# Hybrid S5 and gated linear attention step on one core: plain Strassen operands through late tiles, and a regrouped third group of sweeps

## The chip, the cores and the metric

The kernel runs on one core of a Trainium2 chip. The metric is the device time of one execution in microseconds (us). TensorE (PE) multiplies, VectorE (DVE), ScalarE (ACT) and GpSimd (POOL) do elementwise work, and SyncE (SP) issues most of the DMAs; each engine works through its own instructions in the order of the program. PEld is the load of a matmul's 128x128 stationary operand, which overlaps the matmul before it.

## The reference

One layer with two token mixers, over 1024 prompt tokens and 64 sample tokens (8 sequences of 8), 1088 in all, D_MODEL = 2048, all in float32:

```python
mod = jax.nn.silu(c) @ w_ada + b_ada
shift, scale, gate = jnp.split(mod, 3, axis=-1)
h = rms_norm(x, norm_gain) * (1 + scale[:, None]) + shift[:, None]
u_a, z_a, q, k, v, z_b, g_lr, m_a, m_b = jnp.split(h @ w_in, SPLIT_POINTS, axis=-1)
a_y, sa_re, sa_im = s5_branch(u_a, ...)      # scan, gelu, times sigmoid(g @ w_glu + b_glu)
a_out = (a_y * jax.nn.silu(z_a)) @ w_a_out
b_y, s_gla = gla_branch(q, k, v, log_a, s0_gla, gla_norm_gain)
b_out = (b_y * jax.nn.silu(z_b)) @ w_b_out
merged = jax.nn.sigmoid(m_a) * a_out + jax.nn.sigmoid(m_b) * b_out
y = x + gate[:, None] * (merged @ w_out)     # then a final rms_norm
```

The branch widths are 1024 each; GLA has 4 heads, each with a state of 128x256 that is carried along the sequence.

## The kernel before

Activations stay in SBUF as features by tokens: `h` is 16 tiles of 128 x 1088, each held as a high and a low part (`hh`, `hl`), and every weight tile is split in the same way (`whi` by ACT, `wlo` by DVE). A product is three matmuls per pair of tiles: high by high, low by high, high by low. Instructions are put on the engines in an order that a scheduler has fixed before the run; buffers come from pools with a fixed number per name, and a pool that is opened in the memory of another has to wait until that other one is free.

The program goes through these stages, with their place in the profiled execution in us from the start of the span:

- 0 to 174: norm, the first two thirds of the conditioning vector `mod` (`ada_chunk`, weight tiles `adaraw` of 512 KB, small matmuls on L203), `modulate`, and the first products of `w_in`.
- 174 to 774: S5, the products for v, q and k. During the k products `blocks` prepares the right-hand operands of a Strassen scheme: sums and differences of quarters of `h` ("t1" to "t4"), made by DVE and ACT in a tile `st` (ring of 3) and written to DRAM by L1076, and the plain quarters "11", "21" and "22", which L1079 and L1080 write to DRAM straight from `hh` and `hl`, one DMA of 272 KB for each part.
- 774 to 1998: `sweeps`. Three groups of eight pairs of output tiles; each group has seven sweeps (a11, a12, s1, s2, s3, a22, s4), each of eight products of 48 matmuls of 128x272 (L1176 to L1178). A sweep loads its operand (`hh`, `hl` from `opscr`) while the sweep before runs. `left` loads the weight tiles `raw`, `wraw` and splits them. Behind this the steps of GLA run (`behind`): four units for the samples and sixteen for the prompt, four heads at each of four stretches of 256 tokens. A unit is the chain L777 (decay), L803 and L833 (scores), L842, L874 (`kT`), L934, L941 and L942 (state and output), L951 (norm), with small operations on DVE and ACT between. `next(self.steps, None)` in the product loop places a step; how often is told by `pace`, one number for each sweep. All stores and the loads of the S5 outputs (`yt`, L993) are issued by POOL, the weight loads by SP.
- 1998 to 2100: `branch_a` (gelu of the S5 outputs, `w_glu`).
- 2100 to 2495: `merge` (`w_a_out`, `w_b_out`, 32 products), with the last third of the conditioning (`ada_gates`, weight tiles `gateraw`, L203) stepped between its products.
- 2495 to the end: `final` (`w_out`, residual, norm).

Of the kernel before, what the change touches and what calls it, by code (L numbers as in the profile page):

```python
# [10 lines left out]
F32 = mybir.dt.float32  # L11
F32R = mybir.dt.float32r
U8 = mybir.dt.uint8
AF = mybir.ActivationFunctionType
# [4 lines left out]
P = 128  # L19
# [5 lines left out]
T = TS + TP  # L25
CH = [(0, 320), (320, 384), (704, 384)]
HT = T // 2
# [3 lines left out]
QK4 = 512  # L31


class Hybrid:
# [946 lines left out]


    def stage(self, name):
        return self.p2.tile([P, T], F32, tag="st", name=name, bufs=6)

    def gelu_y(self, i):
        nc = self.nc
# [77 lines left out]
    def blocks(self, h):  # L1065

        nc = self.nc
        V = nc.vector
        with ExitStack() as ctx:
            pp = self.pool("blocks", ctx=ctx)  # L1070

            def split(name, k, v):
                st = pp.tile([P, T], F32R, tag="st", name="st", bufs=3)
                nc.scalar.activation(st[:, :HT], v, AF.Copy)
                V.tensor_tensor(st[:, HT:], v, st[:, :HT].bitcast(F32), ALU.subtract)
                nc.gpsimd.dma_start(self.opscr[name][k], st.bitcast(F32))  # L1076
            for k in range(8):
                for name, (hi, lo), o in (("11", h[8 + k], 0), ("21", h[k], 0), ("22", h[k], HT)):
                    nc.gpsimd.dma_start(self.opscr[name][k][:, :HT], hi[:, o:o + HT].bitcast(F32))  # L1079
                    nc.gpsimd.dma_start(self.opscr[name][k][:, HT:], lo[:, o:o + HT].bitcast(F32))  # L1080
                x, y = (pp.tile([P, T], F32, tag=n, name=n, bufs=2) for n in "xy")
                yield
                V.tensor_tensor(x, h[8 + k][0].bitcast(F32), h[8 + k][1].bitcast(F32), ALU.add)
                V.tensor_tensor(y, h[k][0].bitcast(F32), h[k][1].bitcast(F32), ALU.add)
                b11, b12, b21, b22 = x[:, :HT], x[:, HT:], y[:, :HT], y[:, HT:]
                V.tensor_tensor(b11, b12, b11, ALU.subtract)
                split("t1", k, b11)
                yield
                V.tensor_tensor(b12, b22, b12, ALU.subtract)
                split("t3", k, b12)  # L1090
                V.tensor_tensor(b11, b22, b11, ALU.subtract)
                split("t2", k, b11)
                yield
                V.tensor_tensor(b21, b11, b21, ALU.subtract)
                split("t4", k, b21)
# [37 lines left out]
    def sweeps(self, w, groups, h):  # L1133

        nc = self.nc
# [12 lines left out]
        count = [0, 0]  # L1148

        def raws():  # L1150
            i = count[0] % 10
            count[0] += 1
            if i > 7:
                return self.wp.tile([P, QK4], F32, tag="wraw", name="wraw", bufs=2)
            return rawv[i]

        def fin():
            count[1] += 1
            return finv[count[1] % 8]
        n = 0  # L1160
        for g, group in enumerate(groups):
            for r, (an, bn) in enumerate(self.SWEEPS):
                B, N = sets[n % 2], sets[(n + 1) % 2]
                n += 1
                nxt = self.SWEEPS[r + 1][1] if r < 6 else "11" if g + 1 < len(groups) else None
                for i, (pair, dst, silu) in enumerate(group):
                    ps = self.pmm.tile([P, 2, 512], F32, tag="mm2", name="mm", bufs=2)
                    for q in range(2):
                        hi, lo = self.left(w, an, pair, q, self.wscr[i], raws)
                        for k in range(4):  # L1170
                            c = slice(k * P, (k + 1) * P)
                            bhi, blo = B[4 * q + k]
                            for m in range(2):
                                o = ps[:, m, :NC]
                                bh, bl = bhi[:, m * NC:(m + 1) * NC], blo[:, m * NC:(m + 1) * NC]
                                nc.tensor.matmul(o, hi[:, c], bh, start=q + k == 0, stop=False)  # L1176
                                nc.tensor.matmul(o, hi[:, c], bl, start=False, stop=False)  # L1177
                                nc.tensor.matmul(o, lo[:, c], bh, start=False, stop=q == 1 and k == 3)  # L1178
                            if 4 * q + k in ((), (4,), (2, 6), (1, 4, 6))[self.pace[r]]:
                                next(self.steps, None)  # L1180
                    if nxt:
                        right(nxt, i, N[i])
# [115 lines left out]
    def run(self):  # L1298
        nc, a = self.nc, self.a
# [22 lines left out]
        h = []  # L1322
# [34 lines left out]
        self.pmmctx.close()  # L1357
        self.pmm = self.pool("pmm2", space=PSUM, ctx=self.pmmctx)
        self.steps = self.behind()
        self.pace = (3, 2, 2, 2, 1, 3, 2)  # L1360
        pairs = lambda j0, d, silu=False: [((j0 + i, j0 + i + 1), (d[i], d[i + 1]), silu) for i in range(0, len(d), 2)]
        self.sweeps(w, [pairs(40, self.mas), pairs(56, self.mbs), pairs(8, self.zas, True) + pairs(32, self.zbs, True)], h)
        for _ in self.steps:
# [3 lines left out]
        self.p2ctx = ExitStack()  # L1367
        self.p2 = self.pool("p2", ctx=self.p2ctx)
        aa = self.branch_a()
        self.steps = self.ada_gates()  # L1370
        self.ticks = ()
        self.merge(aa)
        for _ in self.steps:
            pass
        self.final()


# [74 lines left out]
```

## Time and profile before

| | |
|---|---|
| time, median of 3 runs | 2922.17 us (2920.47 to 2926.75) |
| profiled execution | 2938.97 us, span 2937.2 us, mean granted clock 0.982 |
| PE busy | 2813.0 us, 96% of the span |
| PEld busy | 2669.6 us, 91% |
| DVE, ACT, POOL busy | 58%, 35%, 14% |
| DMA | 610.52 MB moved, mean 208 GB/s |

The clock is the rate that the throttle granted to TensorE as a share of full speed: 1.00 is 2.4 GHz, and 1.2 GHz is the other level. A busy share is the mean of the stages, which have different limits. In the windows of the rows below each line gives a stretch, its length, then busy time and count of PE, PEld, DVE, ACT and POOL, then the granted clock, the share of the 16 DMA engines and GB/s. All times of the trace are those of the one profiled execution.

### The profile page before, as it was taken

How to read it: one execution, taken by the hardware profiler on the slowest of the kernel's cores; microseconds unless marked ns; L12 is line 12 of the kernel's file. 1: busy time of each engine (PE TensorE's matmuls, PEld its weight loads, DVE VectorE, ACT ScalarE, POOL GpSimd, SP SyncE). 2: the span in 40 equal slices, each digit the busy share in tenths (PEclk: the TensorE clock that was granted, in tenths of full speed). 3: DMA queues.
4: the chain of work that ended last, by engine and by line, in shares of the span. 5: the costliest groups of instructions: out<-in, count | busy, mean ns of one | idle time of the engine just before them, and what ended most of it. 6: DMA issues, size and time to landing. Idle time of an engine off the chain costs nothing.

```text
span 2937.2 us, 54282 instructions
## 1 busy us (share of the span) xinstructions
PE 2813.0 (96%) x20736; PEld 2669.6 (91%) x20736; DVE 1715.7 (58%) x4016; ACT 1018.9 (35%) x1823; POOL 411.5 (14%) x702
## 2 busy tenths in 40 slices
PE   7999999999899999999999989999999999899987
PEld 4689899999888999998999989999988999899987
DVE  3486777678245786667777535656532322456465
ACT  4222222223233344444344442333221211344434
POOL 1101222121001100011000032011110000203021
PEclk9999999999899999999999999999999999999999
DMA  9944444447668887668867599953575433555455
GB/s 377 386 132 133 117 127 122 114 122 258 235 206 288 295 298 255 187 217 302 292 219 246 194 276 296 319 181 123 173 257 176 136 120 118 184 161 181 145 181 164
DMA packets 321748, 610.52 MB, mean 208 GB/s; under 512 B 47952, under 2 KB 106096, under 8 KB 321360
## 3 DMA queue, kind: packets, MB, share of 16 engines
q1 hardware_dynamic: 256624, 433.51, 46.4%
q0 software_dynamic: 48528, 158.70, 15.6%
q10 hardware_dynamic: 16336, 14.84, 1.5%
q8 instruction: 163, 2.67, 0.4%
q14 instruction: 97, 0.79, 0.1%
HBM read 465.65 MB, written 132.87 MB: 204 GB/s over the span
## 4 chain that ended last, share of the span: by engine, by line
PE 63%; DMA 18%; DVE 8%; issue 7%; ACT 3%; POOL 1%; SPq 1%; DVEq 0%; POOLq 0%; ACTq 0%
PE mm L71 12%; PE mm L72 12%; PE mm L73 12%; PE mm L1178 6%; PE mm L1177 6%; PE mm L1176 6%; DMA raw<-in_w_in_dram 5%; DMA wraw<-in_w_in_dram 2%; DMA hh<-opt 1%; DMA bz<-zbs 1%; DMA raw<-ws 1%; DMA wraw<-in_w_out_dram 1%; PE bg L203 1%; DVE wlo L58 1%; DVE wlo L1130 1%
## 5 line engine op out<-in xcount | busy, mean ns | idle before, releaser
L1176 PE MATMUL mm<-hh,whi 128*128 128x272 f32 x2688 | 788.9, 293 | 25.4 <-ACT whi L1128 13.1
L1178 PE MATMUL mm<-hh,wlo 128*128 128x272 f32 x2688 | 790.2, 294 | 1.6 <-DVE wlo L1130 1.6
L1177 PE MATMUL mm<-hl,whi 128*128 128x272 f32 x2688 | 785.6, 292 | 0.0
L71 PE MATMUL mm<-ahi,whi 128*128 128x384 f32 (+3 forms) x1656 | 547.6, 331 | 17.9 <-DVE y L1248 9.0
L73 PE MATMUL mm<-ahi,wlo 128*128 128x384 f32 (+3 forms) x1656 | 544.2, 329 | 0.6 <-DVE wlo L58 0.4
L72 PE MATMUL mm<-alo,whi 128*128 128x384 f32 (+3 forms) x1656 | 543.5, 328 | 0.0
L1176 PEld LDWEIGHTS mm<-hh,whi 128*128 128x128 f32 x2688 | 514.3, 191 | 31.3 <-ACT whi L1128 14.7
L1178 PEld LDWEIGHTS mm<-hh,wlo 128*128 128x128 f32 x2688 | 513.8, 191 | 5.2 <-DVE wlo L1130 2.4
L1177 PEld LDWEIGHTS mm<-hl,whi 128*128 128x128 f32 x2688 | 514.3, 191 | 3.1 <-issue 1.0
L58 DVE TENSOR_TENSOR wlo<-wraw,whi 128x512 fp32r<-128x512 f32 x368 | 269.5, 740 | 269.8 <-ACT whi L56 268.4
L56 ACT ACTIVATE whi<-wraw 128x512 fp32r<-128x512 f32 x368 | 230.3, 630 | 490.5 <-PE mm L72 278.4
L71 PE MATMUL mm<-hh,whi 128*128 128x384 f32 (+3 forms) x1056 | 344.2, 329 | 9.0 <-ACT hh L266 9.0
L72 PE MATMUL mm<-hl,whi 128*128 128x384 f32 (+3 forms) x1056 | 346.8, 329 | 2.8 <-DVE hl L268 2.8
L73 PE MATMUL mm<-hh,wlo 128*128 128x384 f32 (+2 forms) x1056 | 346.6, 330 | 0.0
L71 PEld LDWEIGHTS mm<-ahi,whi 128*128 128x128 f32 x1656 | 314.6, 190 | 35.2 <-issue 22.8
L73 PEld LDWEIGHTS mm<-ahi,wlo 128*128 128x128 f32 x1656 | 314.5, 190 | 3.9 <-DVE wlo L58 2.5
L72 PEld LDWEIGHTS mm<-alo,whi 128*128 128x128 f32 x1656 | 315.0, 190 | 1.3 <-issue 0.4
L1128 ACT ACTIVATE whi<-raw 128x512 fp32r<-128x512 f32 x270 | 168.6, 628 | 323.3 <-PE mm L1177 191.6
L1130 DVE TENSOR_TENSOR wlo<-raw,whi 128x512 fp32r<-128x512 f32 x270 | 183.9, 684 | 51.4 <-ACT whi L1128 48.6
L71 PEld LDWEIGHTS mm<-hh,whi 128*128 128x128 f32 x1056 | 198.4, 189 | 14.2 <-ACT hh L266 11.5
L72 PEld LDWEIGHTS mm<-hl,whi 128*128 128x128 f32 x1056 | 198.9, 189 | 9.9 <-DVE hl L268 4.7
L73 PEld LDWEIGHTS mm<-hh,wlo 128*128 128x128 f32 x1056 | 198.8, 189 | 3.4 <-issue 2.6
(373 smaller groups left out, 3446.1 us busy)
## 6 DMA issues: line engine op xcount, KB each, us to landing
raw<-in_w_in_dram SPq DMA_DIRECT2D x346, 256.0 KB
wraw<-in_w_out_dram SPq DMA_DIRECT2D x192, 256.0 KB
wraw<-in_w_in_dram SPq DMA_DIRECT2D x182, 256.0 KB
adaraw<-in_w_ada_dram SPq DMA_DIRECT2D x64, 512.0 KB
hl<-opt SPq DMA_DIRECT2D x96, 272.0 KB
hh<-opt SPq DMA_DIRECT2D x96, 272.0 KB
raw<-ws SPq DMA_DIRECT2D x78, 256.0 KB
ws<-raw POOLq DMA_DIRECT2D x77, 256.0 KB, 5.5
```

Source lines behind the costliest of these rows:

```text
L56: nc.scalar.activation(hi, raw, AF.Copy)
L58: nc.vector.tensor_tensor(lo, raw, hi.bitcast(F32), ALU.subtract)
L71: nc.tensor.matmul(ps, hi[:, c], ah[:, sl], start=start, stop=False)
L72: nc.tensor.matmul(ps, hi[:, c], al[:, sl], start=False, stop=False)
L73: nc.tensor.matmul(ps, lo[:, c], ah[:, sl], start=False, stop=stop)
L203: self.nc.tensor.matmul(ps[i:i + 32, :256], self.c32[:, k, :], raw[:, (k - k0) * 256:(k - k0 + 1) * 256], start=k < 4, stop=k >= KT - 4, t ...
L1128: nc.scalar.activation(hi, x, AF.Copy)
L1130: nc.vector.tensor_tensor(lo, x, hi.bitcast(F32), ALU.subtract)
L1176: nc.tensor.matmul(o, hi[:, c], bh, start=q + k == 0, stop=False)
L1177: nc.tensor.matmul(o, hi[:, c], bl, start=False, stop=False)
L1178: nc.tensor.matmul(o, lo[:, c], bh, start=False, stop=q == 1 and k == 3)
```

## The change

Three things change. In `blocks` the plain quarters are copied by ACT into a tile of the ring `st` (two copies each) and written by one DMA of 544 KB, where two DMAs read the activations before. In `sweeps` the pace becomes one list per group; ahead of the third group all GLA steps that are left are drained, and a pool "more" is opened with 12 more weight tiles (`raw2`) and two `gateraw` tiles; in the third group the steps are those of `ada_gates`, in the sweeps a11, a12 and a22; ahead of its last sweep the pool is closed, and the pool of `stage` tiles, in which the S5 outputs are loaded, comes after it. The merge no longer steps anything. The ring of `stage` tiles grows from 6 to 7.

```diff
     def stage(self, name):
-        return self.p2.tile([P, T], F32, tag="st", name=name, bufs=6)
+        return self.p2.tile([P, T], F32, tag="st", name=name, bufs=7)
...
             for k in range(8):
-                for name, (hi, lo), o in (("11", h[8 + k], 0), ("21", h[k], 0), ("22", h[k], HT)):
-                    nc.gpsimd.dma_start(self.opscr[name][k][:, :HT], hi[:, o:o + HT].bitcast(F32))
-                    nc.gpsimd.dma_start(self.opscr[name][k][:, HT:], lo[:, o:o + HT].bitcast(F32))
+                for name, hl, o in (("11", h[8 + k], 0), ("21", h[k], 0), ("22", h[k], HT)):
+                    st = pp.tile([P, T], F32R, tag="st", name="st", bufs=3)
+                    for p in range(2):
+                        nc.scalar.activation(st[:, p * HT:(p + 1) * HT], hl[p][:, o:o + HT].bitcast(F32), AF.Copy)
+                    nc.gpsimd.dma_start(self.opscr[name][k], st.bitcast(F32))
...
         def raws():
-            i = count[0] % 10
             count[0] += 1
+            if sp and count[0] % 2:
+                return sp.tile([P, QK4], F32, tag="raw2", name="raw2", bufs=12)
+            i = (count[0] // 2 if sp else count[0]) % 10
...
+            last = g + 1 == len(groups)
+            if last:
+                for _ in self.steps:
+                    pass
+                sctx = ExitStack()
+                sp = self.pool("more", ctx=sctx)
+                self.p2 = sp
+                self.steps = self.ada_gates()
+            pace = ((1, 2, 2, 2, 2, 3, 2), (3, 3, 2, 2, 2, 3, 2), (2, 2, 0, 0, 0, 1, 0))[g]
...
+                if last and r == 6:
+                    for _ in self.steps:
+                        pass
+                    sp = None
+                    sctx.close()
...
-                            if 4 * q + k in ((), (4,), (2, 6), (1, 4, 6))[self.pace[r]]:
+                            if 4 * q + k in ((), (4,), (2, 6), (1, 4, 6))[pace[r]]:
                                 next(self.steps, None)
...
-        self.pace = (3, 2, 2, 2, 1, 3, 2)
...
         aa = self.branch_a()
-        self.steps = self.ada_gates()
-        self.ticks = ()
         self.merge(aa)
-        for _ in self.steps:
-            pass
```

Three places of the instruction order show what moves. The first is TensorE before the change, at the border between the second group's last sweep (s4, tile `mm_19823`) and the third group's first (a11, tile `mm_19918`); the names `hh`, `hl`, `whi` and `wlo` are sweep operands, `on`, `gr` and `q` belong to GLA:

```order
L1178 MATMUL mm_19823<-hh_1532,wlo_19865 128x272
L1176 MATMUL mm_19918<-hh_1126,whi_19920 128x272
...
L1178 MATMUL mm_19918<-hh_1284,wlo_19922 128x272
L1176 MATMUL mm_19918<-hh_1284,whi_19920 128x272
L1177 MATMUL mm_19918<-hl_1285,whi_19920 128x272
L951 MATMUL bg_19347<-on_19308,ones_h_8747 128x256
L777 MATMUL bg_19360<-gr_19361,wgu_8755 128x256
L803 MATMUL bg_19405<-q_19180,k_19181 32x32 x8
L1178 MATMUL mm_19918<-hh_1284,wlo_19922 128x272
```

The first sweep of the third group follows at once, and the last units of GLA stand among its matmuls. The second is the same border on TensorE after the change (s4 ends with `mm_19836`, a11 begins with `mm_19907`):

```order
L1197 MATMUL mm_19836<-hh_1532,wlo_19874 128x272
L934 MATMUL bg_18152<-v_17473,kT_18111 128x256 x2
...
L951 MATMUL bg_18238<-on_18198,ones_h_8818 128x256
L777 MATMUL bg_18251<-gr_18252,wgu_8826 128x256
...
L951 MATMUL bg_18701<-on_18675,ones_h_8818 128x256
L777 MATMUL bg_18714<-gr_18715,wgu_8826 128x256
...
L951 MATMUL bg_19144<-on_19118,ones_h_8818 128x256
L777 MATMUL bg_19157<-gr_19158,wgu_8826 128x256
...
L951 MATMUL bg_19712<-on_19673,ones_h_8818 128x256
L1195 MATMUL mm_19907<-hh_1126,whi_19910 128x272
```

Seventy rows, all of GLA, now stand between the two sweeps: the end of one unit (from L934) and three whole ones (L777 to L951), with no matmul of a sweep between them. The third place is the queue of SP after the change, at the same border (`o2_204`, `o3_205` are GLA's outputs in DRAM, `on` the tile that is stored, `raw2` the new weight tiles; the brackets name the semaphores that a row waits for):

```order
L956 DMA o2_204<-on_19154 256x1x256 [waits DMAHW3_49,DVE_49]
L945 DMA out_2_dram<-St3_11393 128x256 [waits DMAHW4_49,DVE_49]
L956 DMA o3_205<-on_19722 256x1x256 [waits DMAHW5_49,DVE_49]
L1106 DMA raw2_19908<-in_w_in_dram 128x512 [waits DMAHW4_49,DMAHW3_49,DMAHW5_49,DMAHW2_49,DMAHW6_49,DMAHW1_49,DMAHW7_49,DMAHW0_49,Activation_49]
...
L1106 DMA raw2_19980<-in_w_in_dram 128x512
...
L965 DMA gateraw_20008<-in_w_ada_dram 128x1024 [waits DMAHW2_49,PE_49]
L965 DMA gateraw_20044<-in_w_ada_dram 128x1024 [waits DMAHW3_49,PE_49]
...
L1106 DMA raw2_21058<-in_w_in_dram 128x512 [waits DMAHW6_49,DVE_49]
```

The third group's first weight load stands behind the store of GLA's last output and waits for all eight DMA semaphores; the later `gateraw` loads wait for PE with weight loads behind them.

## Rows read from the trace of the kernel before

**Rows 1.** The page's part 4: the chain that ended last, by engine.
```profile
PE 63%; DMA 18%; DVE 8%; issue 7%; ACT 3%; POOL 1%; SPq 1%; DVEq 0%; POOLq 0%; ACTq 0%
```

**Rows 2.** Windows, 20 to 160 us: busy us, clock, DMA share, GB/s.
```profile
60.00:80.00 20.00, 18.29 (x132) 12.94 (x132) 6.96 (x18) 3.95 (x5) 4.27 (x8) 1.00 1.02 405
...
sum 140.00, PE 122.91 PEld 79.72 DVE 62.28 ACT 41.98 POOL 23.72; mean PE 17.56 PEld 11.39 DVE 8.90 ACT 6.00 POOL 3.39
```

**Rows 3.** Line L1080, the second of the two copy DMAs of `blocks`.
```profile
L1080 POOL DMA_DIRECT2D op<-hl x24: 540/540/542, 51.1 to 172.8; - x24
```

**Rows 4.** Windows of 20 us around the start of the sweeps.
```profile
780.00:800.00 20.00, 14.57 (x89) 11.35 (x88) 7.48 (x30) 7.82 (x19) 1.63 (x3) 0.74 0.52 162
800.00:820.00 20.00, 13.53 (x71) 11.56 (x72) 7.32 (x22) 7.68 (x16) 0.32 (x1) 0.70 0.48 147
```

**Rows 5.** Line L1076, the other DMAs of `blocks`.
```profile
L1076 POOL DMA_DIRECT2D opt<-st x32: 531/531/561, 673.4 to 747.8; - x32
```

**Rows 6.** Line L1074, the copy on ScalarE ahead of each of them.
```profile
L1074 ACT ACTIVATE st<-x x24: 643/659/662, 670.9 to 742.6; 128x544 fp32r<-128x544 f32 x24
```

**Rows 7.** Windows: the first sweep, the second group, the third group.
```profile
774.00:855.80 81.80, 69.90 (x474) 62.52 (x473) 29.82 (x91) 31.11 (x67) 1.95 (x4) 0.83 0.54 168
...
1205.60:1623.30 417.70, 402.59 (x3981) 388.43 (x3980) 294.45 (x724) 189.83 (x386) 41.32 (x73) 0.99 0.75 248
1623.30:1998.20 374.90, 353.90 (x2845) 350.04 (x2844) 205.98 (x339) 142.39 (x201) 70.79 (x130) 0.98 0.78 250
```

**Rows 8.** Timeline of the last GLA unit: start, duration, engine, line, operation, idle before.
```profile
1634.10 0.59 PE L951 MATMUL bg<-on,ones_h 128*128 128x256 f32 x2
...
1658.90 0.38 ACT L876 ACTIVATE kT<-bg 128x256 f32<-128x256 f32 x1 [2.39 <-PE bg L874]
...
1661.69 1.02 PE L934 MATMUL bg<-v,kT 128*128 128x256 f32 x4
...
1663.65 0.48 DVE L943 SCALAR_TENSOR_TENSOR St<-St,eb,bg 128x256 f32<-128x256 f32 x1 [2.64 <-PE bg L942]
...
1666.54 0.38 PE L942 MATMUL bg<-q,St 128*128 128x128 f32 x2
...
1668.14 0.74 POOL L948 TENSOR_TENSOR on<-on 128x256 f32<-128x256 f32 x1 [36.37 <-ACT on L947]
...
1671.21 0.59 PE L951 MATMUL bg<-on,ones_h 128*128 128x256 f32 x2
...
1677.70 0.69 DVE L955 TENSOR_TENSOR on<-bg,rsn 128x512 f32<-128x512 f32 x1
...
1678.42 0.52 SPq L956 DMA_DIRECT2D o<-on  x1
```

**Rows 9.** Page, parts 5, 6: a weight split; a DMA, us to landing.
```profile
L1128 ACT ACTIVATE whi<-raw 128x512 fp32r<-128x512 f32 x270 | 168.6, 628 | 323.3 <-PE mm L1177 191.6
...
ws<-raw POOLq DMA_DIRECT2D x77, 256.0 KB, 5.5
```

**Rows 10.** Windows: sweeps a11, s1, a22 and s4 of the third group.
```profile
1623.30:1680.60 57.30, 57.30 (x541) 55.93 (x540) 30.63 (x74) 27.31 (x52) 2.01 (x3) 1.00 0.51 170
...
1737.30:1793.60 56.30, 50.51 (x384) 50.12 (x385) 24.82 (x38) 21.24 (x24) 20.54 (x39) 0.94 0.97 289
...
1898.50:1946.80 48.30, 48.30 (x387) 48.30 (x386) 24.90 (x38) 15.38 (x24) 3.78 (x7) 1.00 0.73 244
1946.80:1998.20 51.40, 48.43 (x386) 47.86 (x385) 38.74 (x54) 27.53 (x31) 13.97 (x25) 1.00 0.51 157
```

**Rows 11.** Windows: 14 products of the merge with gates, 14 without.
```profile
2099.50:2303.00 203.50, 197.70 (x1282) 174.81 (x1282) 72.86 (x113) 45.36 (x59) 19.51 (x37) 0.98 0.65 219
2303.00:2469.00 166.00, 166.00 (x1009) 166.00 (x1008) 49.83 (x77) 32.48 (x42) 11.08 (x21) 1.00 0.36 116
```

**Rows 12.** Groups by line, 2099.5 to 2303 us: the gates' matmuls.
```profile
L203 PE MATMUL bg<-gateraw,c 128*32 128x256 f32 x256 | 22.1, 397 | 2.9 <-DMA gateraw<-in_w_ada_dram 2.9
```

**Rows 13.** Line L993, the loads of the S5 outputs.
```profile
L993 POOL DMA_DIRECT2D yt<-y x64: 528/531/896, 1683.3 to 1987.6; - x64
```

More of the change, by code (lines that the diff above doesn't have):

```diff
@@ L1164, in sweeps @@
                 n += 1
+                if last and r == 6:
+                    for _ in self.steps:
+                        pass
+                    sp = None
+                    sctx.close()
                 nxt = self.SWEEPS[r + 1][1] if r < 6 else "11" if g + 1 < len(groups) else None
```

## The prediction

> **What bounds the kernel now.** I read the chain that ended last first, then windows of stages, then the rows around the places that change. The chain is TensorE for 63% and DMA for 18% of the span [rows 1]; an edit pays only where TensorE waits or runs work of low value, and costs only where it makes TensorE wait. Four such places are touched. In the first stage the 16 DMA engines are full (share 1.02, 405 GB/s from 60 to 80 us), yet PE is busy 122.9 of the 140 us from 20 to 160 [rows 2]. At the start of the sweeps PE is busy 14.6 and 13.5 of 20 us, at a clock of 0.74 and 0.70 [rows 4]; this first sweep takes 81.8 us [rows 7]. A sweep without disturbance takes 48.3 us, as a22 of the third group shows, while s1 takes 56.3 at a DMA share of 0.97 and a11 57.3 with GLA in it [rows 10]. In the merge 14 products with gates between them take 203.5 us, 14 without take 166.0 [rows 11].
>
> **The change, part by part.** The sum is made against the profiled 2938.97 us, which is 16.8 us above the median of the runs; I carry the difference over to the median unchanged.
>
> *Early copies gone.* L1080 issues 24 DMAs from 51.1 to 172.8 us [rows 3], L1079 as many in the same way. Each moves 0.279 MB; spread evenly, some 27 of the 48 lie before 120 us, 7.5 MB, or 19 us of the DMA engines at 405 GB/s. But PE stands idle only 140 − 122.9 = 17.1 us there [rows 2], and part of that is the chain of modulation, which no DMA shortens. Gain between 0 and 17; I take 12.
>
> *Late copies.* 48 copies of 0.66 us [rows 6] go to ACT, 31.6 us, beside a PE that works through the k products; ACT has room. The ring is what paces them: 32 uses took 673.4 to 747.8 us, 2.40 us each [rows 5]. At that pace 56 uses end at about 673 + 55 × 2.4 = 805 instead of 748. Behind it on ACT stand the weight splits of the first sweep's second product, and the pool that GLA needs opens later. So PE stalls some 17 us between 780 and 805; but it already loses 5.4 + 6.5 us there, and part of its clock, to the first GLA units, which now start later [rows 4]. One stall takes the place of the other: 0, between −10 and +15. GLA loses about 40 us of cover, though.
>
> *GLA out of the third group.* The second group takes 417.7 us [rows 7], 79.6 over seven sweeps of 48.3; it holds most of the units. The new paces place about as many steps in the two groups together as before (248 against 240), and since they start later, nearly as many units get done: −3, between −8 and +2.
>
> *The drain.* This is the decisive part. The order of TensorE after the change has the end of one unit and three whole ones between the second and the third group, without a sweep matmul among them; before, they lay among the products of a11. So the third group can't start until GLA has run through by itself, at the speed of its own chain over DVE, ACT and PE. The nearest rows are those of the last unit before: from one L951 at 1634.1 to the next at 1671.2, 37.1 us [rows 8]. In that time its small matmuls stood in PE's queue behind sweep matmuls: `kT` was ready at 1659.28 and L934 began at 1661.69 (2.4 us); the state at 1664.13, L942 at 1666.54 (2.4); POOL's result at 1668.88, L951 at 1671.21 (2.3). Without these 7.1 us it takes 30.0. Four weight splits of 0.63 us on ACT [rows 9] lie in its way too, which leaves 27.5; more waits of the first kind lie earlier in the unit, while a slower clock (below) would lengthen its matmuls. I take 25, between 22 and 30. The end of the first unit, L934 to L951, was 9.5 us, less two waits of 4.7: 5. Behind the last L951 comes the norm until the output is ready, 1671.21 to 1678.39, 7.2 us [rows 8]; then its store, then the first `raw2` load, which waits for that store, then a split of 0.63. A DMA of this size takes 5.5 us to land among others [rows 9]; for the pair I take 7.5, between 4 and 11. So the drain costs 5 + 3 × 25 + 7.2 + 7.5 + 0.6 = 95 us, between 5 + 66 + 12 = 83 and 5 + 90 + 19 = 114. Nothing covers it: PE, with 96% busy elsewhere, has only these matmuls.
>
> A rule of the Trainium skill bears on the pair of transfers: "DMA: Bandwidth & Descriptors", section "Anatomy of one DMA — SWDGE (gpsimd) path", gives about 2.0 us plus the bytes over 436 GB/s, an estimate of 2.6 us for 256 KB and 5.2 for the pair. The row's 5.5 us for one is twice that, in traffic; by the page the sum would be 2.3 us smaller.
>
> *Third group.* Before: 374.9 us [rows 7]. After, seven sweeps at 48.3 are 338; the gates' matmuls, 22.1 us [rows 12] and an estimated 3 for their transposes, move in: 363. Of the 8 us that s1 lost at a DMA share of 0.97 [rows 10], and the sweeps before and after it likewise, I keep half, 12 or 13: the S5 loads leave, the gates' 16.8 MB come. That is 376, +1 to +2, taken as +2, between −10 and +25.
>
> *S5 outputs late.* The 64 loads, 0.53 us of POOL each [rows 13], were spread from 1683 on. Now all 34 us of them stand in or behind a last sweep of 51.4 us [rows 10], the last ones behind the sweep's stores, and the gelu and splits behind them; `branch_a` runs k-outer, and needs the last tiles late. +3, between 0 and +15.
>
> *Merge.* 203.5 − 166.0 = 37.5 us [rows 11], of which 22.1 are the gates' matmuls [rows 12] and 5.8 PE's idle time; the rest is what lies around small matmuls. The branch's loads may still stall. −34, between −24 and −37.5.
>
> Sum: −12 + 0 − 3 + 95 + 2 + 3 − 34 = +51. On the median: 2922 + 51 = **2973**.
>
> **The rivals.** *The drain is short.* The three units belong to three heads and share no data, so their work on DVE and ACT could overlap. Against it: in the order each L777 stands behind the L951 of the unit before, and the chain starts at L777. The other parts give −44 together, so the kernel is faster by more than 0.2% (5.8 us, about what a measurement here tells from no change) once the drain costs under 38; with units of 5 us it is 5 + 15 + 15 = 35, and the time 2913; with none left it is 2878.
>
> *The third group becomes bound by DMA.* It moved 250 GB/s for 374.9 us [rows 7], 94 MB; without the S5 loads (4.5 MB) and with the gates it is 106 MB. At s1's 289 GB/s for 0.97 [rows 10], 298 at full share, this takes 356 us, just below the 376 allowed; on SP, a `gateraw` load that waits for PE holds the weight loads behind it, with only 12 more tiles as cover. If it decides, +25 instead of +2: 2996.
>
> *The drain at the lower clock.* With PE busy some 14 of 20 us the granted clock was 0.70 to 0.74 [rows 4], a mix of 2.4 and 1.2 GHz. The drain leaves PE far less busy, so its matmuls could all run at 1.2 GHz: units of 30 us, a drain of 110, time 2988. The Trainium skill warns of this in "TensorE: Matmul & The Clock Gate", section "HAM oscillation — how this bites in real kernels": waits between bursts of matmuls cost the clock at the start of each burst. By that page this rival is the likelier course within my range of units; the trace shows the lower clock at such a place, but no drain.
>
> *The early copies weren't in the way.* If stage one is held by PE and modulation alone, the first term is 0: 2985.
>
> **How the numbers follow.** The forecast with its own range, 2950 to 2995, has 0.58; it holds the last two rivals. The third group bound by DMA, or several costs at their upper ends, 2995 to 3025, has 0.17. A drain somewhat shorter, or gains at their bounds, 2928 to 2950, has 0.08. Within 0.2%: 0.05. Faster: 0.12. Slower is 0.83. The bounds, added in squares (drain 17, copies early 9 and late 13, third group 18, the rest 14), give some 32 us to each side; with the rival of DMA above and part of the short drain below, 2918 to 3012 holds 8 in 10.
>
> **What would show it.** Between the second and the third group a stretch of some 95 us in which PE holds only GLA's lines, at a low clock. Units of about 25 us from L951 to L951. The first `raw2` load some 8 us ahead of the first a11 matmul, and behind the last GLA store. The merge at about 11.9 us a product from the start. Stage one at about 162 instead of 174 us. L1076 ending past 800, the first sweep about as long as before. The prediction is wrong if the drain is under 50 us, if DMA is at full share throughout the third group, or if stage one or the first sweep moves by more than 20.

## The result and the profile after

The changed kernel takes 2962.39 us (2961.43 to 2966.74, 4 runs) against 2922.76 of the kernel before: a ratio of 1.0137, 95% interval 1.0119 to 1.0155. It is slower by some 40 us, where 51 were forecast.

The windows of the stages after the change (columns as in the rows ahead of the prediction): the first sweep; the rest of the first two groups; the gap; the third group; `branch_a`; the merge.

```profile
761.10:829.60 68.50, 55.86 (x410) 54.51 (x409) 24.46 (x61) 29.05 (x58) 6.42 (x12) 0.88 0.77 263
829.60:1594.90 765.30, 743.37 (x6890) 710.83 (x6890) 514.19 (x1240) 315.86 (x631) 79.22 (x143) 0.99 0.79 263
1594.90:1691.40 96.50, 33.90 (x424) 26.19 (x422) 51.10 (x157) 40.22 (x85) 3.42 (x5) 0.60 0.20 71
1691.40:2065.40 374.00, 368.61 (x2959) 349.38 (x2960) 188.41 (x298) 119.64 (x176) 55.09 (x102) 0.99 0.81 275
2065.40:2162.70 97.30, 96.33 (x580) 95.25 (x579) 61.58 (x64) 37.49 (x51) 20.58 (x38) 1.00 0.47 140
2162.70:2543.10 380.40, 380.08 (x2306) 379.47 (x2305) 145.53 (x198) 87.61 (x110) 42.54 (x73) 1.00 0.45 145
```

The first profile of the kernel before lay 16 us above its usual runs, so I had it profiled again (below); that second profile, with a span of 2924.6 us, is the one to compare with. Its windows, in the same order, without a gap:

```profile
778.10:856.80 78.70, 69.45 (x474) 62.07 (x473) 29.87 (x91) 30.96 (x67) 1.95 (x4) 0.85 0.56 172
856.80:1616.60 759.80, 743.39 (x7091) 712.98 (x7091) 534.02 (x1295) 332.96 (x667) 80.42 (x144) 1.00 0.80 264
1616.60:1989.90 373.30, 353.21 (x2845) 349.62 (x2844) 206.58 (x339) 142.61 (x201) 70.72 (x130) 0.99 0.78 251
1989.90:2085.80 95.90, 95.44 (x579) 95.15 (x578) 55.76 (x59) 26.13 (x46) 6.44 (x12) 1.00 0.35 114
2085.80:2499.50 413.70, 409.33 (x2578) 386.63 (x2577) 144.44 (x215) 91.33 (x118) 42.20 (x72) 1.00 0.52 171
```

(In the first profile of the kernel before the merge ran from 2094 to 2511 us, not from 2100 to 2495 as the list of stages ahead of the prediction has it.)

So the 40 us are a sum of large terms: the sweeps start at 761.1 instead of 778.1 (−17.0), the first sweep −10.2, the rest of the first two groups +5.5, the gap +96.5, the third group +0.7, `branch_a` +1.4, the merge −33.3; `final` is shorter by 3. The gap is a stretch that was not there before: TensorE is busy 33.9 of 96.5 us, at a mean granted clock of 0.60.

One unit of GLA in the gap, on TensorE (start, duration, engine, line, operation, idle before and what ended it):

```profile
1599.86 1.22 PE L951 MATMUL bg<-on,ones_h 128*128 128x256 f32 x2 [1.55 <-POOL on L948]
1600.52 0.77 PE L777 MATMUL bg<-gr,wgu 96*128 96x256 f32 x1
...
1612.29 0.73 PE L833 MATMUL bg<-g 128*32 128x16 f32 x32 [10.63 <-DVE g L820]
...
1619.79 2.07 PE L934 MATMUL bg<-v,kT 128*128 128x256 f32 x4 [0.47 <-ACT kT L876]
...
1626.62 0.83 PE L951 MATMUL bg<-on,ones_h 128*128 128x256 f32 x2 [1.55 <-POOL on L948]
1626.97 0.69 PE L777 MATMUL bg<-gr,wgu 96*128 96x256 f32 x1
```

From one L777 to the next are 26.5 us. Two fifths of it are one wait: from L803 to L833 TensorE stands for 10.6 us until DVE and ACT have made the decays. L934, 1.02 us in [rows 8], takes 2.07 here, at the lower clock. Over a whole unit, from one L951 to the next, TensorE's GLA matmuls took 6.23 us before, at a granted clock of 1.00:

```profile
1634.10:1671.20 37.10, 6.23 (x133) 5.07 (x134) 4.38 (x14) 1.92 (x4) 1.00 0.33 97
```

In the gap they take 10.45, at 0.55 (both windows count the instructions on GLA's tile `bg` alone, and have no column for POOL):

```profile
1626.62:1653.18 26.56, 10.45 (x134) 8.06 (x134) 4.39 (x14) 1.93 (x4) 0.55 0.09 29
```

TensorE's waits over the whole gap (us, times, longest):

```profile
PE bg L833 <- DVE g L820: 36.5, 9, 10.7
PE mm L1195 <- ACT whi L1130: 12.0, 1, 12.0
```

The second line is the way out. It is seen in the chain that ended last (start, duration, what): norm of the last output, its store, then the load, then the first split and the first matmul.

```profile
1678.66 0.71 PE bg L951 x2
...
1683.40 0.70 DVE on L955
1684.12 2.41 DMA o<-on
1687.13 3.56 DMA gateraw<-in_w_ada_dram
1690.69 0.63 ACT whi L1130
```

The last L951 ends the GLA work at 1678.66; the output is ready at 1684.1, the first new weight tile is issued when its store has landed, at 1686.7, and TensorE goes on at 1691.4: 12.7 us. (The chain names a `gateraw` load, issued right behind the first weight tile; the split reads the weight tile, so I take the wait to be for that.) The list of stages has all stores issued by POOL; these stores of GLA's outputs are issued by SP, so the last of them and the first weight load stand in one queue.

In the first stage the DMA engines are no longer full from 60 us on:

```profile
60.00:80.00 20.00, 18.67 (x131) 12.38 (x125) 6.57 (x16) 3.22 (x5) 0.00 (x0) 1.00 0.89 352
...
sum 140.00, PE 125.09 PEld 84.91 DVE 67.96 ACT 44.45 POOL 0.00; mean PE 17.87 PEld 12.13 DVE 9.71 ACT 6.35 POOL 0.00
```

They stood at a share of 1.02 before [rows 2]. The copies that took the place of the early DMAs, and the end of `blocks`:

```profile
L1081 ACT ACTIVATE st<-hh x24: 639/658/662, 651.9 to 774.0; 128x544 fp32r<-128x544 f32 x24
```

```profile
L1076 POOL DMA_DIRECT2D opt<-st x32: 531/531/542, 660.3 to 788.3; - x32
```

The last one starts at 788 us, where it was 748 [rows 5]. In the first sweep TensorE waits twice for weight splits, 5.5 and 7.2 us:

```profile
PE mm L1195 <- ACT whi L1130: 12.6, 2, 7.2
```

The first of these splits, at 775.07, stood behind the copies on ACT. For the second ACT itself was idle, until a weight tile had landed, from loads that SP issued from 776.4 us on, behind a wait of 6.5 us for the splits before:

```profile
790.70 1.17 ACT L1130 ACTIVATE whi<-raw 128x512 fp32r<-128x512 f32 x2 [3.42 <-DMA raw<-in_w_in_dram]
```

At that time the DMA engines were full, and TensorE had nothing to do:

```profile
784.00:791.00 7.00, 0.21 (x2) 0.00 (x0) 0.72 (x1) 0.96 (x2) 0.53 (x1) 0.74 1.03 417
```

So one wait is ACT's order, the other the load on the DMA engines; whose transfers filled them was not taken apart, but with the early copies both waits go (below).

The third group loads more than before, and TensorE hardly waits; its sweep s1:

```profile
1812.20:1861.60 49.40, 49.40 (x394) 48.84 (x393) 26.47 (x41) 10.77 (x17) 9.18 (x17) 1.00 0.99 366
```

The S5 outputs are loaded from 2010 us on, and were from 1683 [rows 13]:

```profile
L993 POOL DMA_DIRECT2D yt<-y x64: 528/531/793, 2009.8 to 2083.1; - x64
```

The merge runs its 32 products at the pace of those without gates in [rows 11], 11.9 us each.

### The profile page after: what moved, and what is told of

It is laid out like the page before. It is cut to its first block, busy times and chain, and to the rows that moved or that the text cites. A ratio compares the mean times of both kernels' runs of the same rounds, so it can differ in the third digit from the quotient of the medians.

```text
span 2964.8 us, 54310 instructions
## 1 busy us (share of the span) xinstructions
PE 2805.0 (95%) x20736; PEld 2672.4 (90%) x20736; DVE 1728.4 (58%) x4016; ACT 1043.8 (35%) x1867; POOL 398.3 (13%) x678
## 4 chain that ended last, share of the span: by engine, by line
PE 62%; DMA 12%; issue 8%; DVE 7%; ACT 3%; POOL 2%; SPq 0%; DVEq 0%; POOLq 0%; ACTq 0%
PE mm L71 11%; PE mm L73 11%; PE mm L72 11%; PE mm L1195 8%; PE mm L1197 8%; PE mm L1196 8%; DMA raw<-in_w_in_dram 4%; DMA wraw<-in_w_in_dram 2%; DMA wraw<-in_w_out_dram 1%; DMA bz<-zbs 1%; DVE wlo L1132 1%; DVE wlo L58 1%; POOL yt L993 1%; DMA hh<-opt 1%; DVE s L295 1%
## 5 line engine op out<-in xcount | busy, mean ns | idle before, releaser
L71 PE MATMUL mm<-hh,whi 128*128 128x384 f32 (+2 forms) x1056 | 344.1, 329 | 4.0 <-ACT hh L266 4.0
L1130 ACT ACTIVATE whi<-raw 128x512 fp32r<-128x512 f32 x283 | 177.1, 629 | 427.8 <-PE mm L1196 349.4
L1132 DVE TENSOR_TENSOR wlo<-raw,whi 128x512 fp32r<-128x512 f32 x283 | 193.0, 686 | 133.3 <-ACT whi L1130 91.6
```

Source lines behind the costliest of these rows:

```text
L71: nc.tensor.matmul(ps, hi[:, c], ah[:, sl], start=start, stop=False)
L1130: nc.scalar.activation(hi, x, AF.Copy)
L1132: nc.vector.tensor_tensor(lo, x, hi.bitcast(F32), ALU.subtract)
```

## The experiments

Ratios are to the kernel before, run on the same chip as the experiment in question; its medians there were 2926.6 to 2927.9 us.

**The kernel before, once more** (no edit).

> The kernel before, unchanged, profiled a second time. The two profiles differ by 27.6 us of span while the medians of the runs differ by 39.6, so some 12 us of the first profile of before are not in its usual runs. Theory 1: they lie in its first sweep, which took 81.8 us there; a second profile shows that sweep at about 68 to 70 us, as after the change, and a span of some 2922. Theory 2: they are spread over the whole program (clock); then the first sweep takes 81 to 82 us again and every stage is a little shorter.

Time 2926.43, span 2924.6; the first sweep took 78.7 us, as the second group of windows above shows. Theory 1 falls: the first profile was 4 us faster ahead of the sweeps, 12 slower in them and 3 in the merge, so its excess has no one place, as theory 2 has it in part. The comparison of stages above is with this profile.

**Only the plain operands** (in the kernel before, the edit to `blocks` alone, as in the diff of the change).

> The kernel before with the change to the plain operands alone. Theory 1 (the early copies held the first stage, the late ones are hidden): the start of the sweeps moves from 774 to 761 us, the first sweep stays at what it is in the second profile of before, and the time is 2923 - 13 = 2910. Theory 2 (the late copies give it back in the first sweep, whose weight splits stand behind them on ScalarE, and in GLA, which starts some 30 us later): 2923 to 2930.

Ratio 0.9997 (0.9983 to 1.0012): no change, though the sweeps start at 760.6. The windows are the first sweep, the rest of two groups, the third group:

```profile
760.60:844.90 84.30, 63.94 (x442) 58.46 (x443) 31.47 (x87) 36.74 (x70) 6.48 (x13) 0.86 0.71 231
844.90:1607.40 762.50, 742.88 (x6989) 712.68 (x6988) 526.47 (x1268) 322.16 (x652) 80.40 (x143) 0.99 0.79 264
1607.40:1988.10 380.70, 360.50 (x2977) 355.64 (x2977) 220.33 (x388) 152.76 (x228) 71.75 (x131) 0.98 0.78 249
```

Of the 17.5 us won ahead of the sweeps, 5.6 go in the first sweep, 2.7 in the rest of two groups and 7.4 in the third, where GLA, which began later, ends later: its last L951 stands at 1695 us instead of 1665, and the S5 loads, which wait for its memory, begin at 1712 instead of 1676. Theory 2.

**The change with early copies.**

```diff
-                for name, hl, o in (("11", h[8 + k], 0), ("21", h[k], 0), ("22", h[k], HT)):
-                    st = pp.tile([P, T], F32R, tag="st", name="st", bufs=3)
-                    for p in range(2):
-                        nc.scalar.activation(st[:, p * HT:(p + 1) * HT], hl[p][:, o:o + HT].bitcast(F32), AF.Copy)
-                    nc.gpsimd.dma_start(self.opscr[name][k], st.bitcast(F32))
+                for name, (hi, lo), o in (("11", h[8 + k], 0), ("21", h[k], 0), ("22", h[k], HT)):
+                    nc.gpsimd.dma_start(self.opscr[name][k][:, :HT], hi[:, o:o + HT].bitcast(F32))
+                    nc.gpsimd.dma_start(self.opscr[name][k][:, HT:], lo[:, o:o + HT].bitcast(F32))
```

> The changed kernel with the plain operands written early, straight from the activations, as before the change. Theory 1 (the late copies save 13 to 18 us before the sweeps; they gave it back in the other experiment only because GLA, which starts later, held memory longer; here GLA runs out in the gap either way): 2962 + 15 = 2977. Theory 2 (GLA's earlier start shortens the gap): 2962 or less.

Ratio 1.0116 (1.0091 to 1.0142), not to be told from the change's 1.0137. Both theories fail, the second by its mechanism, though its time is met: the gap is as long as before (1595.5 to 1691.9), and the 14 us that the early copies cost ahead of the sweeps come back at once in the first sweep:

```profile
775.50:830.60 55.10, 52.99 (x417) 51.28 (x418) 17.23 (x44) 21.15 (x44) 1.63 (x3) 0.97 0.59 186
```

55.1 us instead of 68.5: this is the 12.6 us wait for the splits, gone (1.4 us are left). The late copies move a cost, they don't remove it.

**The paces alone** (the kernel before with the change's numbers for the first two groups).

```diff
         for g, group in enumerate(groups):
+            pace = ((1, 2, 2, 2, 2, 3, 2), (3, 3, 2, 2, 2, 3, 2), (3, 3, 3, 2, 1, 3, 2))[g]
...
-                            if 4 * q + k in ((), (4,), (2, 6), (1, 4, 6))[self.pace[r]]:
+                            if 4 * q + k in ((), (4,), (2, 6), (1, 4, 6))[pace[r]]:
```

> The kernel before with the paces of the change in the first two groups (GLA goes on at three steps a product in the third). Theory 1 (it is the lighter pace of the first sweep, one step a product instead of three, that made this sweep 13 to 24 us shorter): the first sweep falls from 79 to about 55 us, the third group grows by one more unit, some 9 us, and by later S5 loads, and the time falls by about 10, to 2915. Theory 2 (the first GLA units cost the same wherever they stand): no change.

Ratio 1.0075 (1.0058 to 1.0093), slower, which neither theory allowed. The profiled run lies 7 us under the median. First sweep, rest of two groups, third group:

```profile
777.50:850.10 72.60, 63.89 (x444) 58.37 (x443) 25.77 (x76) 30.54 (x65) 1.95 (x4) 0.86 0.57 178
850.10:1620.10 770.00, 748.50 (x6894) 716.90 (x6893) 514.41 (x1222) 314.86 (x623) 80.26 (x143) 0.98 0.78 260
1620.10:2002.20 382.10, 364.22 (x3072) 358.17 (x3071) 229.96 (x427) 162.83 (x250) 71.36 (x131) 0.99 0.78 249
```

The first sweep gains 6 us, not 24: the scheduler packed the first unit as tightly as before (L777 at 777.5 and 813.7), where in the kernel with early copies the same paces spread it (775.1 to 859.4). The rest of two groups loses 10, the third group 9. So the pace alone doesn't explain the 55 us. Where the scheduler places GLA goes with it: the first sweep has 384 matmuls of its own, so 33 of GLA's stand in it with the early copies, 60 here and 90 in the kernel before. That this placing is the cause is not shown, nor why the scheduler chose otherwise here.

**The loop alone** (the kernel before, with the steps run out ahead of the third group, and no pool behind it).

```diff
         for g, group in enumerate(groups):
+            if g + 1 == len(groups):
+                for _ in self.steps:
+                    pass
```

> The kernel before with one thing of the change: the loop that runs out GLA's steps ahead of the third group, without a pool behind it. Theory 1 (the gap is made by the memory of the new pool, and the loop only decides in which order the program is written): the scheduler interleaves as before, no change, within 0.3%. Theory 2 (the loop itself makes the third group wait): 1.7 units of 26 us in a gap instead of some 9 us among the sweeps, 2924 + 35 = 2959.

Ratio 0.9988 (0.9977 to 1.0000): theory 1. The instructions of GLA still stand among those of a11; there is no gap (1613.8, the last matmul of one group, to 1613.8).

**One unit less in the gap.**

```diff
-            pace = ((1, 2, 2, 2, 2, 3, 2), (3, 3, 2, 2, 2, 3, 2), (2, 2, 0, 0, 0, 1, 0))[g]
+            pace = ((2, 3, 3, 3, 3, 3, 3), (3, 3, 3, 3, 3, 3, 3), (2, 2, 0, 0, 0, 1, 0))[g]
```

> The changed kernel with more GLA steps in the first two groups (paces 2,3,3,3,3,3,3 and 3 throughout); the order then has 2.25 units between the groups instead of 3.25. Theory 1 (each unit in the gap costs 26.5 us, among the sweeps some 8.5): 2962 - 18 = 2944. Theory 2 (a unit costs the same wherever it stands): 2962, within 6.

Ratio 1.0066 (1.0044 to 1.0088), 0.0071 below the change's, 21 us; theory 1 (18). The gap, now shorter by 25.8 us:

```profile
1602.30:1673.00 70.70, 24.76 (x291) 19.21 (x289) 36.02 (x108) 27.91 (x58) 2.71 (x4) 0.61 0.23 81
```

**No new weight tiles.**

```diff
         def raws():
             count[0] += 1
-            if sp and count[0] % 2:
-                return sp.tile([P, QK4], F32, tag="raw2", name="raw2", bufs=12)
-            i = (count[0] // 2 if sp else count[0]) % 10
+            i = count[0] % 10
```

> The changed kernel without the 12 weight tiles: all weights go through the old ring, only the gates' tiles lie in GLA's memory. The order then has three products of a11 among GLA's end, with one of the 3.25 units, and the rest of it ahead of the fourth. Theory 1 (the first weight tile's wait for GLA's memory makes the gap, and the gate tiles' wait would make one too, a little later): the gap shrinks by 13 us of exit and some 18 of cover, so 2930 to 2938 if the old ring is enough. Theory 2 (the 12 tiles are what keeps a11 and a12 fed): the sweeps of the third group lose 8 us each as before the change, and the time is 2960 or more.

Ratio 1.0099 (1.0073 to 1.0126): 11 us better than the change, where I expected 24 to 32. There is no gap between the groups, but a11 takes 149.7 us instead of 61.0. TensorE's waits in it:

```profile
PE bg L833 <- DVE g L820: 26.9, 9, 10.7
PE bg L203 <- DMA gateraw<-in_w_ada_dram: 15.5, 4, 11.3
```

The gates' first matmuls wait for the same memory as the weight tiles did, and stand in TensorE's order behind all of GLA. Only the first products of a11 moved ahead of it, with the end of one unit and the first step of the next; I had counted a whole unit there. So either kind of tile makes the gap. Of the sweeps behind a11 only s2 loses as theory 2 had it, 56.6 us against 48.2; that is what the 12 tiles are worth here.

**The gates back in the merge** (the change with `self.steps = self.ada_gates()` ahead of the merge as before, 6 stage tiles).

> The changed kernel with the gates stepped in the merge again, as before the change, and with 6 stage tiles (7 don't fit there with the gate tiles); the pool of 12 weight tiles and the gap ahead of the third group stay. Theory 1 (moving the gates pays only what stalls around them in the merge): the merge gets its 37 us back, the third group loses the 29 us by which a11, a12 and a22 exceed 48.3 now, so 2962 + 8 = 2970. Theory 2 (the gates are hidden in the third group): the merge's 37 come back and the third group stays at 374, 2999. Theory 3 (the gates' loads cost more there than they cost in the merge): under 2962.

Ratio 1.0201 (1.0170 to 1.0232): 19 us slower than the change. Third group and merge:

```profile
1687.60:2043.10 355.50, 345.37 (x2688) 344.19 (x2689) 187.86 (x285) 120.82 (x172) 60.73 (x112) 0.98 0.76 248
2141.60:2557.20 415.60, 407.50 (x2561) 386.63 (x2560) 143.71 (x214) 89.51 (x117) 41.19 (x70) 1.00 0.51 168
```

The merge takes 35.2 us more, `final` 4.7 more, the third group 18.5 less: moving the gates, with the seventh stage tile that it allows, is worth about 19 us, between theories 1 and 2. I expected 8, from a third group 29 us shorter; its first six sweeps are 25 shorter, but the last takes 60.4 us instead of 53.9, and why it does stays open.

**The pool later.** GLA goes on among a11, a12 and s1 of the third group, and the pool opens ahead of s2:

```diff
-            if last:
-                for _ in self.steps:
-                    pass
-                sctx = ExitStack()
-                sp = self.pool("more", ctx=sctx)
-                self.p2 = sp
-                self.steps = self.ada_gates()
-            pace = (..., (2, 2, 0, 0, 0, 1, 0))[g]
+            pace = (..., (3, 3, 3, 2, 2, 1, 0))[g]
             for r, (an, bn) in enumerate(self.SWEEPS):
...
+                if last and r == 3:
+                    for _ in self.steps:
+                        pass
+                    sctx = ExitStack()
+                    sp = self.pool("more", ctx=sctx)
+                    self.p2 = sp
+                    self.steps = self.ada_gates()
```

> The changed kernel, but GLA goes on through the sweeps a11, a12 and s1 of the third group (three steps a product), and the pool with the 12 weight tiles and the gates opens ahead of s2; gates in s2, s3 and a22. Theory 1 (the 96.5 us between the groups are a wait for GLA's memory, at the wrong place): the third group follows at once, the 3.25 units cost some 8 to 10 us each among the sweeps, about 30, and the time is 2962 - 96 + 30 = 2896, under the kernel before. Theory 2 (what is left of GLA costs its 26 us a unit wherever it stands, since DVE and ACT are needed for the weight splits too): 2962 - 13 = 2949, only the exit of the pool is saved. Theory 3 (gates and the S5 loads then fill the DMA engines in s2 and s3): 2910 to 2925.

Ratio 0.9947 (0.9929 to 0.9964), 2912.65: faster than both kernels. The gap is gone. The first three sweeps together, then s2:

```profile
1596.20:1768.70 172.50, 167.38 (x1576) 162.88 (x1575) 110.45 (x252) 88.95 (x157) 21.01 (x38) 1.00 0.75 253
1768.70:1843.40 74.70, 60.05 (x487) 52.19 (x486) 32.69 (x54) 11.27 (x19) 4.30 (x8) 0.91 0.94 336
```

172.5 us for three sweeps with 3.25 units, against 149.7 in the kernel with the gates back (50.9, 48.9, 49.9): 7 us a unit instead of 26.5, although these three sweeps don't have the 12 weight tiles yet, so theory 2 falls. But s2 takes 74.7, as theory 3 has it, without the S5 loads: those start behind it, at 1957.7. TensorE waits there for the gates' loads:

```profile
PE bg L203 <- DMA gateraw<-in_w_ada_dram: 12.3, 2, 7.5
```

**Gates in s3 and a22 only** (pace 3, 3, 3, 0, 3, 2, 0 in the third group).

> The late pool again, with no gates in s2, three steps a product in s3 and two in a22 (before: two, two, one from s2 on). Theory 1 (s2 took 74.7 us because the gates' loads found the DMA engines full there): s2 falls to some 56, s3 and a22 stay near 48.3 plus 0.7 us for each step, 65 and 59, and the time falls by 10 to 12, to about 2901. Theory 2 (the loads stall wherever they are, since only two tiles are there for them): no gain, 2913.

Ratio 0.9915 (0.9884 to 0.9946). The sweeps s2, s3, a22:

```profile
1768.00:1817.90 49.90, 49.86 (x385) 49.89 (x386) 29.92 (x47) 9.43 (x15) 3.39 (x7) 0.97 1.01 358
1817.90:1891.50 73.60, 67.08 (x546) 54.80 (x545) 29.90 (x52) 17.49 (x28) 3.78 (x7) 0.93 0.84 289
1891.50:1954.30 62.80, 60.62 (x496) 52.51 (x495) 27.41 (x46) 16.69 (x28) 4.47 (x9) 0.97 0.79 265
```

s2 is free of stalls, but s3 and a22 now exceed what their steps should cost by some 8 and 3 us: in this profile the third group is only 3 us shorter, and the stall went with the loads:

```profile
PE bg L203 <- DMA gateraw<-in_w_ada_dram: 6.1, 5, 2.2
```

That speaks for theory 2. But the profiled run, 2912.17 us, was the slowest of the four; the ratio is 9 us better than the first late pool's, close to theory 1's 10 to 12, and the two intervals meet. So the stall is shown to have moved; what that did to the time is not settled.

**Five gate tiles.** The same paces; 6 new weight tiles and 5 gate tiles in the same memory.

```diff
-                raw = self.p2.tile([P, 1024], F32, tag="raw", name="gateraw", bufs=2)
+                raw = self.p2.tile([P, 1024], F32, tag="raw", name="gateraw", bufs=5)
...
-                return sp.tile([P, QK4], F32, tag="raw2", name="raw2", bufs=12)
+                return sp.tile([P, QK4], F32, tag="raw2", name="raw2", bufs=6)
```

> The late pool with no gates in s2, three steps a product in s3, two in a22, and the same memory shared out otherwise: 6 new weight tiles and 5 gate tiles instead of 12 and 2. Theory 1 (with two tiles the gates' loads can't run ahead, so s3 and a22 stall by 8 and 3 us): s3 and a22 fall from 73.6 and 62.8 to 65 and 59, and the time by about 10, ratio to before 0.988. Theory 2 (the loads take from the weights what the DMA engines have, whatever the tiles): no gain, or a loss where six weight tiles are too few, ratio 0.992 to 0.997.

Ratio 0.9893 (0.9877 to 0.9909), 2896.18 us: the lowest of all, 31 us under the kernel before, though its interval meets that of the experiment before it. s2, s3 and a22:

```profile
1767.30:1820.70 53.40, 53.40 (x450) 50.27 (x449) 25.87 (x40) 9.39 (x14) 5.41 (x10) 1.00 0.93 335
1820.70:1884.70 64.00, 59.61 (x514) 54.45 (x513) 37.16 (x63) 17.58 (x31) 3.77 (x7) 0.97 0.97 358
1884.70:1940.70 56.00, 56.00 (x465) 50.95 (x464) 25.87 (x44) 16.41 (x27) 4.52 (x9) 1.00 0.78 271
```

At a DMA share of 0.93 and 0.97 TensorE is busy 53.4 of 53.4 and 59.6 of 64.0 us: the loads run ahead, and TensorE's idle time is 4 us in all instead of 9 (6.5 and 2.2 above). No wait for a gate tile is left; the longest of those that are (1750 to 2000 us):

```profile
PE mm L1195 <- ACT whi L1130: 3.6, 3, 1.9
```

The stalls follow theory 1. Gate tiles and weight tiles were changed together, so what the six fewer weight tiles did is not told apart.

**The gates in the merge, with the late pool** (12 weight tiles, 6 stage tiles).

> The late pool with the 12 weight tiles alone; the gates go back into the merge, with 6 stage tiles. Theory 1 (in the late pool the gates cost the third group 41 to 46 us, more than the 35 that the merge is spared): the third group falls from 412 or 415 to 370 to 375, the merge grows by 35, and the time is that of the late pools or some 5 us less, ratio 0.990. Theory 2 (the weight tiles and the gates' loads fight for the same DMA engines only in s2 and s3, and the merge stalls as before): ratio 0.995 to 1.000.

Ratio 0.9956 (0.9936 to 0.9976). Third group and merge:

```profile
1591.90:1970.20 378.30, 366.71 (x3110) 361.84 (x3110) 233.53 (x436) 170.83 (x262) 65.52 (x119) 0.98 0.75 250
2068.00:2482.30 414.30, 407.52 (x2562) 386.36 (x2561) 143.85 (x214) 89.66 (x117) 41.18 (x70) 1.00 0.51 168
```

Against the first late pool the third group is 36.6 us shorter, the merge 33.6 longer: with two gate tiles, stepped as there, the move earns nothing, as theory 2's ratio says. (With no gates in s2 the two tiles reached 0.9915, some 12 us under this; the intervals meet.) With five the third group takes 396.5 us, 18 more than here, for the 33 that the merge is spared: now it pays, by 18 us in the ratio.

## Why the prediction held

The time, 2962, is in the range and in the forecast's own range of 2950 to 2995; the sum was 11 us too high. The main part, a stretch between the groups in which GLA runs alone, came as described. By its terms, measured against the second profile of the kernel before; the sum was built on the first, and the unchanged kernel differs between the two by 4 us at the start of the sweeps, 3 in the first sweep and 8 in the rest of the first two groups, so a smaller difference of two profiles says little:

- *The drain*: forecast 95, measured 96.5. It was put together from 5 (measured 5.0 from L934 to L951), three units of 25 (26.3 on average) and an exit of 15 (12.7). The rival of a short drain fell: the units did not overlap, each L777 stands behind the L951 of the unit before.
- *The drain's units* fit in part by luck. They are the row of [rows 8], at full clock, without its waits; the lower clock was left as a rival with units of 30. That clock came (0.50 to 0.63 in windows of 20 us). By the two windows of a unit above it made GLA's matmuls 4.2 us longer; if all of them stand in the chain, a unit of 26.6 us would have taken some 22 at full clock, by this estimate. So 25 was up to 3 us too long for the unit that it described, and the clock made up for it. "HAM oscillation — how this bites in real kernels" in the Trainium skill's "TensorE: Matmul & The Clock Gate" describes waits for DMA between bursts of matmuls that cost the clock; here the waits are for DVE and ACT, and the trace agrees, with L934 at 2.07 instead of 1.02 us.
- *The drain's exit* was 3 us too long: the norm took 5.5 instead of 7.2, and for the pair of transfers I took 7.5 us. The store took 2.6 to the next issue and the load 3.9 until its split, 6.6, between that and the 5.2 estimated from the Trainium skill's "DMA: Bandwidth & Descriptors", section "Anatomy of one DMA — SWDGE (gpsimd) path"; but that section is on DMAs that GpSimd issues, and SP issues both of these. The first weight load stands 4.6 us ahead of the first matmul, not 8.
- *What makes it*: I blamed the order and the wait of the first `raw2` load. The loop alone does nothing, and without the new weight tiles the gate tiles wait in their place: it is the memory of GLA, opened to tiles that are needed at once. Moved behind GLA's end it costs 7 us a unit instead of 26.5.
- *Early copies gone*: forecast −12, measured −17.0 to the start of the sweeps (−12.9 against the first profile, −14 by the kernel with early copies). The bound was taken from TensorE's idle time; that fell only from 20.0 to 14.9 us between 20 and 220 us. The granted clock, 0.91 from 80 to 100 and from 120 to 140 us in the first profile, was 1.00 there after the change; how much of the gain it makes was not worked out.
- *Late copies*: forecast 0, from a PE stall of 17 us in the place of losses to the first GLA units. Measured −10.2 for the first sweep (−13.3 against the first profile), just beyond the bound of −10. The stall is there, 12.6 us, since `blocks` ended at 788 and not at 805; 7.2 of it is a wait for a weight load among full DMA engines, where I had named only ACT's order. What GLA had cost this sweep was more than the 12 us that I let the stall replace: with the early copies, and 33 of GLA's matmuls in it, the sweep takes 55.1 us, some 24 less. This step was sized wrongly. Part of its gain is work that now stands later: 26 of GLA's matmuls are left in the sweep, of 90. With the paces alone the sweep doesn't shorten so, hence what part the pace has in it stays open.
- *GLA out of the third group*: forecast −3, measured +5.5 for the rest of the first two groups, beyond its bound of +2; against the first profile it is −2.2. The two profiles of the kernel before leave open which it is.
- *Third group*: forecast +2, measured +0.7; gates in, S5 loads out, as said. It is not bound by DMA: that rival took 298 GB/s as the most, and s1 moved 366 with TensorE busy throughout. In the late pool, where GLA leaves fewer sweeps for the gates, it came true in s2.
- *S5 outputs late*: +3 forecast; `branch_a` +1.4.
- *Merge*: −34 forecast, −33.3 measured (−36.7 against the first profile); the stalls around the gates went with them. Net of what the gates cost in the third group the move is worth 19 us, the seventh stage tile included.

The 11 us between forecast and result are the first sweep (10), the early copies (5) and `final` (3), against the first two groups, which came out 8 us above the forecast. So the total is close partly because errors of both signs met.

## What to carry over

A pool opened in memory that background work still holds is a wait for the end of that work. Where the tiles in it are needed at once, by loads whose users stand in the order of the busiest engine, the whole leftover runs alone, at the length of its own chain: here 26 us a unit instead of 7. Open it behind the last use, by the order of the engine and not by the order of the code. And when loads are moved under work that already fills the DMA engines, give them tiles enough to run ahead. With two gate tiles the move earned nothing in one order (0.9947 against 0.9956) and perhaps 12 us in another (0.9915); with five, and six weight tiles fewer, it earned 18 (0.9893).

## What the runs showed of the hardware

ACT reloaded its tables four times in each GLA unit of the gap, 1.28 us each (ahead of L133, a square root, L781, an exponential, L782, a logarithm, and L857, an exponential): three of them stand in the chain of every unit, some 4 of its 26.5 us. The granted clock was 0.50 in the first 20 us in which TensorE had only GLA's matmuls (1600 to 1620, busy 5.6 us), and 0.90 again in the 20 us behind the gap, with TensorE busy throughout. The DMA engines moved 366 GB/s at a share of 0.99 in the third group's s1 after the change, and 289 at 0.97 in its s1 before [rows 10]: a share near 1 is not one rate.
